# Per-token-tile products of a two-layer hybrid encoder trunk moved from GpSimd to ScalarE

## The chip, the cores and the metric

The kernel runs on one core of a Trainium2 chip. The metric is the device time of one execution in microseconds (us), and the time of a version is the median over several executions. Engines are named as the profile names them: PE is TensorE, DVE is VectorE, ACT is ScalarE, POOL is GpSimd, SP is SyncE.

## The reference

Two layers of an encoder with D = 2048 run over 768 tokens: one request of 256 and one of 512. In each layer an RMS norm and one wide projection feed four groups of heads, four heads each: A (gated delta rule in both directions over chunks), B (differential attention), C (short gated convolution) and M (cross-attention into 256 memory tokens). Their outputs are gated, concatenated, projected, normed and added to the input.

```python
for l in range(DEPTH):                                   # DEPTH = 2
    h = _rmsnorm(x, norm_pre[l])
    (a_qkv, a_dec, a_beta, a_z, b_q, ..., m_q, m_z) = split(h @ w_in[l])
    y_a = _gdn_branch(a_qkv, a_dec, a_beta, a_z, ...)    # group A
    y_b = _diff_branch(b_q, b_k, b_v, b_z, ...)          # group B
    y_c = _conv_branch(c_b, c_c, c_x, c_z, conv_w[l])    # group C
    y_m = _memory_branch(m_q, m_z, mem, ...)             # group M
    y = concat([y_a, y_b, y_c, y_m]) @ w_out[l]
    x = x + _rmsnorm(y, norm_post[l])
# group A, per head and direction, k and q of unit length
decay  = exp(where(tri_incl, g_i - g_j, -inf))           # g: running sum of the decay
a_low  = where(tri_strict, (k * beta) @ k.T * decay, 0)
u      = solve(a_low + eye, v * beta)
```

At the end of a head of A or B its output is normed over the head's 128 columns: every token's row is multiplied by one root of its own.

## The kernel before, in words

**Tiles.** The 768 tokens are 6 token tiles of 128 (`NCH` = 6). A per-head array such as `A`, `U`, `ao` or `bo` has shape [128, 6, 128]: one row of partitions for each token of a tile, six tiles side by side. A factor "per row and token tile" is a small [128, 6] array.

**Projections.** All large products run in split precision: a weight of 512 rows by 128 columns (a quarter) is cast by ACT to a rounded `hi` (L171), DVE subtracts that to get `lo` (L182), and PE multiplies hi and lo by the activations, 24 matmuls for a quarter (L221). `run_jobs` walks over these quarters in a fixed order; quarter i issues the cast of quarter i+4 and, further ahead, its load.

**Head work as tasks.** What the heads do besides projecting is written as generators. Between two quarters `tick` lets the tasks go on by one step, `yield` ends a step. So the small work of several heads is interleaved with the projections in one program order, and each engine executes its part of that order strictly in turn: an instruction that waits for a semaphore holds up all behind it on its engine.

**The three places of the change.** In `head_norm_out` (tasks of A and B) DVE forms the root `hny` in a chain of small operations, the output `ao` or `bo` is multiplied by it (L610), and PE transposes the result (L619), in two groups of four and two token tiles. In `gdn` the masks are multiplied by decays (`gm`, L680; four products of a head, a high and a low part for each of two directions); PE sums them over a triangle (L691), ACT takes the exponential into `A` (L692). Later DVE makes `nD`, a product of beta and key norms (L722, L723), and `U` is `A` times `nD` for both directions (L726).

**A neighbour.** Group M's task runs between them. For each pair of token tiles PE makes scores in a PSUM tile (L1152), DVE their maximum `mmx` (L1155, L1156), ACT two exponentials `mE` (L1159), which are the last readers of that PSUM tile, DVE divides by the sum (L1163, L1165), PE transposes (L1171), ACT and DVE copy the transpose to a high and a low part `mPT` (L1173, L1174), and PE multiplies them by the memory values (L1182). PSUM tiles for these small products come from a pool of four.

Of the kernel before, what the change touches and what calls it, by code (L numbers as in the profile page):

```python
# [12 lines left out]
AF = mybir.ActivationFunctionType  # L13
ALU = mybir.AluOpType
# [4 lines left out]
P = 128  # L19
# [4 lines left out]
NCH = T // P  # L24
# [62 lines left out]
class Trunk:  # L87
# [504 lines left out]
    def head_norm_out(self, o, c, w, st, l, yi):  # L592

        nc = self.nc
        yield 0
        sq = self.sc("hsq")
        nc.scalar.activation(sq[:, :T], o.rearrange("p n c -> p (n c)"), AF.Square)
        yield 0
        so = self.small(NCH, "so")
        nc.vector.tensor_reduce(so, sq[:, :T].rearrange("p (n c) -> p n c", n=NCH), AX.X, ALU.add)  # L600
        yield 0
        if c is not None:
            c2 = self.small(NCH, "c2")
            nc.vector.tensor_tensor(c2, c, c, ALU.mult)
            nc.vector.tensor_tensor(so, so, c2, ALU.mult)
        nc.vector.tensor_scalar(so, so, 1.0 / P, EPS, ALU.mult, ALU.add)  # L606
        r = self.rsqrt(so, NCH, "hn")
        if c is not None:
            nc.vector.tensor_tensor(r, r, c, ALU.mult)
        nc.gpsimd.tensor_tensor(o, o, r.unsqueeze(2).to_broadcast([P, NCH, P]), ALU.mult)  # L610
        while "g" not in st:
            yield 0
        y = st["g"]
        yield (2, 1)
        pts = []
        for off, ln, n0, nn in GROUPS:
            pt = self.psl()
            for n in range(nn):
                nc.tensor.transpose(pt[:, n * P:(n + 1) * P], o[:, n0 + n, :], self.ident)  # L619
            pts.append(pt)  # L620
        for (off, ln, n0, nn), pt in zip(GROUPS, pts):
            nc.vector.scalar_tensor_tensor(y[:, off:off + ln], pt[:, :ln], w, y[:, off:off + ln], ALU.mult, ALU.mult)
        yield from self.store_y(l, yi, y)
# [46 lines left out]
    def gdn(self, l, h, st):  # L670
        nc = self.nc
        while l not in self.dec:
            yield 0
        dec = self.dec[l]
        masks = (self.LE, self.GE)
        gms = []
        for d in range(2):
            gms.append([self.scr("gm") for _ in range(2)])
            for x in range(2):
                nc.gpsimd.tensor_tensor(gms[d][x].rearrange("p (n c) -> p n c", n=NCH),  # L680
                                        masks[d].unsqueeze(1).to_broadcast([P, NCH, P]),
                                        dec["gs"][:, x, 2 * h + d, :].unsqueeze(2).to_broadcast([P, NCH, P]), ALU.mult)
        A = []
        for d in range(2):
            yield (2, 1)
            a = self.sc3("A")
            af = a.rearrange("p n c -> p (n c)")
            for off, ln, n0, nn in GROUPS:
                pt = self.psl()
                for x in range(2):  # L690
                    nc.tensor.matmul(pt[:, :ln], self.maskr[:, d, :], gms[d][x][:, off:off + ln], start=x == 0, stop=x == 1)  # L691
                nc.scalar.activation(af[:, off:off + ln], pt[:, :ln], AF.Exp)  # L692
            sg = 1 - 2 * d
            nc.gpsimd.affine_select(a, a, pattern=[[0, NCH], [sg, P]], compare_op=ALU.is_ge,  # L694
                                    fill=0.0, base=0, channel_multiplier=-sg)
            A.append(a)
        while "k" not in st:
            yield 0
        k = st["k"]
        yield 2  # L700
        ktok = self.sc3("ktok")
        ss = self.small(12, "ss")
        sq = self.sc("ksq")
        for off, ln, n0, nn in GROUPS:
            pt = self.psl()
            for n in range(nn):
                nc.tensor.transpose(pt[:, n * P:(n + 1) * P], k[:, n0 + n, :], self.ident)
            nc.scalar.copy(ktok[:, n0:n0 + nn, :].rearrange("p n c -> p (n c)"), pt[:, :ln])
        nc.scalar.activation(sq[:, :T], ktok.rearrange("p n c -> p (n c)"), AF.Square)
        yield 0  # L710
        nc.vector.tensor_reduce(ss[:, 0:6], sq[:, :T].rearrange("p (n c) -> p n c", n=NCH), AX.X, ALU.add)
        nc.vector.tensor_scalar(ss[:, 0:6], ss[:, 0:6], 4.0 * EPS, None, ALU.add)
        rk = self.rsqrt(ss[:, 0:6], 6, "kn")
        nE = self.small(6, "nE")
        nc.vector.scalar_tensor_tensor(nE, ss[:, 0:6], -0.5, rk, ALU.mult, ALU.mult)
        rk2 = self.small(6, "rk2")
        nc.vector.scalar_tensor_tensor(rk2, rk, -1.0, rk, ALU.mult, ALU.mult)
        nD = self.small(12, "nD").rearrange("p (d n) -> p d n", d=2)
        nDR = self.small(12, "nDR").rearrange("p (d n) -> p d n", d=2)
        U = []  # L720
        for d in range(2):
            nc.vector.tensor_tensor(nD[:, d, :], dec["be"][:, 2 * h + d, :], rk2, ALU.mult)  # L722
            nc.vector.tensor_tensor(nDR[:, d, :], nD[:, d, :], dec["eR"][:, 2 * h + d, :], ALU.mult)  # L723
        for d in range(2):
            u = self.sc3("U")
            nc.gpsimd.tensor_tensor(u, A[d], nD[:, d, :].unsqueeze(2).to_broadcast([P, NCH, P]), ALU.mult)  # L726
            U.append(u)
        yield 0
        while "q" not in st:
            yield 0  # L730
        q = st["q"]
        for p in range(3):
            yield 1
            pt = self.psl()
            p4 = pt.rearrange("p (a n c) -> p a n c", a=2, n=2)
            for j in range(2):
                n = 2 * p + j
                for a, x in enumerate((k, q)):
                    nc.tensor.matmul(p4[:, a, j, :], k[:, n, :], x[:, n, :])  # L739
            for X, a in ((U, 0), (A, 1)):  # L740
                for d in range(2):
                    v = X[d][:, 2 * p:2 * p + 2, :]
                    nc.vector.tensor_tensor(v, p4[:, a], v, ALU.mult)
        inv = Task(self.gdn_inverse(U, st))
        self.tasks.append(inv)
        yield 2
        sq = self.sc("qsq")
        for off, ln, n0, nn in GROUPS:
            pt = self.psl()
            for n in range(nn):  # L750
                nc.tensor.transpose(pt[:, n * P:(n + 1) * P], q[:, n0 + n, :], self.ident)
            nc.scalar.activation(sq[:, off:off + ln], pt[:, :ln], AF.Square)
        yield 0
        nc.vector.tensor_reduce(ss[:, 6:12], sq[:, :T].rearrange("p (n c) -> p n c", n=NCH), AX.X, ALU.add)
        nc.vector.tensor_scalar(ss[:, 6:12], ss[:, 6:12], 4.0 * EPS, None, ALU.add)
        rq = self.rsqrt(ss[:, 6:12], 6, "qn")
        cq = self.small(6, "cq")
        nc.vector.tensor_scalar(cq, rq, P ** -0.5, None, ALU.mult)
        while "v" not in st:
            yield 0  # L760
        v = st["v"]
        yield 2
        nv = self.sc3("nv")
        for off, ln, n0, nn in GROUPS:
            pt = self.psl()
            for n in range(nn):
                nc.tensor.transpose(pt[:, n * P:(n + 1) * P], v[:, n0 + n, :], self.ident)
            nc.vector.tensor_tensor(nv[:, n0:n0 + nn, :], pt[:, :ln].rearrange("p (n c) -> p n c", n=nn),
                                    nE[:, n0:n0 + nn].unsqueeze(2).to_broadcast([P, nn, P]), ALU.mult)
        while "inv" not in st:  # L770
            yield 0
        o = self.sc3("ao")
        yield from self.gdn_scan(h, dec, k, q, ktok, nv, U, A, nD, nDR, o)
        yield from self.head_norm_out(o, cq, self.gnw[:, l:l + 1], st, l, h)
# [774 lines left out]
```

## Time and profile before

| what | value |
|---|---|
| median of 3 executions | 3085.11 us (3083.47 to 3088.78) |
| the profiled execution | 3081.02 us, its span 3079.3 us |
| busy share of the span: PE, DVE, ACT, POOL | 97%, 52%, 29%, 28% |
| mean granted clock of PE | 0.989 of full speed |
| HBM | 87 GB/s over the span |

The span is the time from the first to the last instruction of the profiled execution; 1.7 us of its own time lie around it. Busy shares are means over the whole span. In rows of the trace the first number is the start and the second the duration, in us; "x4" is the number of instructions merged into a row; brackets at the end tell how long the engine had stood idle before the row, and what ended that.

### The profile page before, as it was taken

Reading aid. Unit: us, or ns where it says so; the run is one execution under the profiler, and the core shown is the slowest. Engines: PE = TensorE matmul, PEld = TensorE weight load, DVE = VectorE, ACT = ScalarE, POOL = GpSimd, SP = SyncE. Lnnn points to the kernel's source line nnn. Section 1 sums busy time; section 2 is a strip of 40 time slices with the busy share of each in tenths; the row PEclk is TensorE's granted clock in tenths of the full one; section 3 lists DMA queues with packets and bytes.
Section 4 is the critical chain, followed back from the end, with each engine's and each line's share of the span. In section 5 each row is a group of like instructions: output and inputs, shape, how many; then the busy total and the mean of one; then the engine's idle time right before and its main releaser. Section 6 shows DMA issues by size and latency. Waiting matters only on the chain. (4 is left out here: it accounts for less than half of the span.)

```text
span 3079.3 us, 47114 instructions
## 1 busy us (share of the span) xinstructions
PE 2998.0 (97%) x18606; PEld 2600.5 (84%) x18606; DVE 1610.6 (52%) x2964; ACT 902.2 (29%) x1802; POOL 861.4 (28%) x1070
## 2 busy tenths in 40 slices
PE   8899999999999999999989999999999999999997
PEld 6788888888888888888867888888888888888886
DVE  7755465455355645632596554645463546455236
ACT  6432222222222232421234222322222222334111
POOL 4316114310701250311253260252107014303014
PEclk9999999999999999999999999999999999999998
DMA  7422223122222221531473222221222122224226
GB/s 246 124 69 64 66 58 84 52 64 73 71 55 69 73 61 46 181 96 56 128 241 104 69 61 62 63 79 54 71 75 65 53 69 72 61 74 156 59 66 215
DMA packets 170829, 269.81 MB, mean 88 GB/s; under 512 B 41584, under 2 KB 54128, under 8 KB 170608
## 3 DMA queue, kind: packets, MB, share of 16 engines
q1 hardware_dynamic: 169376, 265.74, 29.1%
q8 instruction: 146, 2.39, 0.3%
q10 hardware_dynamic: 1232, 1.07, 0.1%
q14 instruction: 75, 0.61, 0.1%
HBM read 233.97 MB, written 32.77 MB: 87 GB/s over the span
## 5 line engine op out<-in xcount | busy, mean ns | idle before, releaser
L221 PE MATMUL pp<-h,hi 128*128 128x512 f32 (+1 forms) x9600 | 2178.1, 344 | 9.8 <-ACT h L365 6.2
L221 PEld LDWEIGHTS pp<-h,hi 128*128 128x128 f32 x9600 | 1507.1, 189 | 232.1 <-issue 8.3
L221 PE MATMUL pp<-h,lo 128*128 128x512 f32 (+1 forms) x4800 | 1309.2, 342 | 8.8 <-DVE lo L182 8.8
L182 DVE TENSOR_TENSOR lo<-raw,hi 128x512 fp32r<-128x512 f32 x700 | 607.5, 880 | 742.7 <-ACT hi L171 739.7
L221 PEld LDWEIGHTS pp<-h,lo 128*128 128x128 f32 x4800 | 762.0, 189 | 122.9 <-DVE lo L182 12.4
L171 ACT CAST hi<-raw 128x512 fp32r<-128x512 f32 x700 | 415.9, 618 | 247.0 <-PE pp L221 192.1
L1355 POOL TENSOR_TENSOR acc<-acc,osq 128x768 f32<-128x768 f32 (+2 forms) x36 | 53.7, 1492 | 407.2 <-ACT osq L1348 407.2
L797 POOL TENSOR_TENSOR tl<-ul 48x30 f32<-48x30 f32 (+14 forms) x240 | 136.3, 568 | 94.4 <-DMA ul<-ud 34.3
L799 POOL TENSOR_TENSOR ul<-ul,tl 48x30 f32<-48x30 f32 (+14 forms) x240 | 145.1, 605 | 18.8
L610 POOL TENSOR_TENSOR ao<-ao,hny 128x768 f32<-128x768 f32 x8 | 13.2, 1646 | 481.5 <-DVE so L606 435.8
L1340 DVE TENSOR_SCALAR ys<-pp,npost_s 128x768 f32<-128x768 f32 (+2 forms) x41 | 34.4, 839 | 187.6 <-PE pp L221 187.6
L1073 ACT ACTIVATE E<-s,bmx 128x512 f32<-128x512 f32 (+1 forms) x96 | 58.4, 613 | 235.6 <-DVE bmx L1072 224.8
L648 DVE SCALAR_TENSOR_TENSOR cva<-cv,gconv_s,cva 128x770 f32<-128x770 f32 x96 | 104.5, 1088 | 5.0
L1348 ACT ACTIVATE osq<-pp 128x768 f32<-128x768 f32 (+2 forms) x38 | 25.8, 678 | 260.2 <-DVE ys L1340 260.2
L680 POOL TENSOR_TENSOR gm<-masks_s,gr 128x768 fp32r<-128x768 f32 x32 | 51.8, 1648 | 116.9 <-DVE gr L566 116.9
L726 POOL TENSOR_TENSOR U<-A,nD 128x768 f32<-128x768 f32 x16 | 27.4, 1733 | 166.9 <-DVE nD L722 166.9
L924 ACT ACTIVATE x<-s,nD 128x128 f32<-128x128 f32 x96 | 33.6, 367 | 137.1 <-PE s L922 116.7
L1072 DVE TENSOR_REDUCE bmx<-s 128x1 f32<-128x512 f32 (+1 forms) x96 | 53.2, 596 | 28.9 <-PE s L1069 28.5
L610 POOL TENSOR_TENSOR bo<-bo,hny 128x768 f32<-128x768 f32 x8 | 13.3, 1665 | 186.3 <-DVE hny L298 186.3
L1159 ACT ACTIVATE mE<-s,mmx 128x256 f32<-128x256 f32 x48 | 22.4, 471 | 139.8 <-DVE mmx L1156 131.6
L694 POOL TENSOR_SCALAR_AFFINE_SELECT A<-A 128x768 f32<-128x768 f32 x16 | 14.8, 926 | 171.4 <-ACT A L692 171.4
L587 ACT ACTIVATE gate<-pp 128x768 f32<-128x768 f32 x32 | 26.0, 812 | 125.3 <-PE pp L221 124.6
(304 smaller groups left out, 2703.8 us busy)
## 6 DMA issues: line engine op xcount, KB each, us to landing
raw<-wu SPq DMA_DIRECT2D x472, 256.0 KB, 3.0
raw<-wo SPq DMA_DIRECT2D x164, 256.0 KB, 3.4
raw<-wkv SPq DMA_DIRECT2D x64, 256.0 KB, 4.6
y<-gate SPq DMA_DIRECT2D x24, 384.0 KB, 2.6
mem<-memT SPq DMA_DIRECT2D x32, 256.0 KB, 4.7
x<-xT SPq DMA_DIRECT2D x16, 384.0 KB, 6.9
yl<-y SPq DMA_DIRECT2D x24, 256.0 KB, 5.3
xl<-xT SPq DMA_DIRECT2D x16, 384.0 KB, 4.4
```

Of the source, the lines that this page charges most:

```text
L171: nc.scalar.copy(hi, rf)
L182: nc.vector.tensor_tensor(lo, rf, hi.bitcast(F32), ALU.subtract)
L221: nc.tensor.matmul(job.ps[:, o:o + n], w[:, j, :], job.H[g][k][:, x, :], start=(k == 0 and w is hi and x == 0), stop=(k == KT - 1 and w is ...
L648: nc.vector.scalar_tensor_tensor(a, cb[:, i:i + 770], w[:, i:i + 1], a, ALU.mult, ALU.add)
L680: nc.gpsimd.tensor_tensor(gms[d][x].rearrange("p (n c) -> p n c", n=NCH), masks[d].unsqueeze(1).to_broadcast([P, NCH, P]), dec["gs"][:, x, ...
L797: nc.gpsimd.tensor_tensor(t, ul[:, j + 1:, j:j + 1].to_broadcast([48, m, j]), ul[:, j:j + 1, 0:j].to_broadcast([48, m, j]), ALU.mult)
L799: nc.gpsimd.tensor_tensor(ul[:, j + 1:, 0:j], ul[:, j + 1:, 0:j], t, ALU.add)
L924: nc.scalar.activation(xt[:, ci, :], pb[:, ci * P:(ci + 1) * P], AF.Copy, scale=nD[:, d, n:n + 1])
L1072: nc.vector.tensor_reduce(mx[:, j:j + 1], pts[j][:, :ln], AX.X, ALU.max, negate=True)
L1073: nc.scalar.activation(E[j], pts[j][:, :ln], AF.Exp, bias=mx[:, j:j + 1], accum_out=sm[:, j:j + 1])
L1340: nc.vector.tensor_scalar(st["ys"][m][:, a:b], ps[:, a:b], self.npost[:, l, m:m + 1], None, ALU.mult)
L1355: nc.gpsimd.tensor_tensor(acc[:, o:o + n], acc[:, o:o + n], sq[:, o:o + n], ALU.add)
```

## The change

All 64 POOL products of the three places (32 `gm`, 16 `U`, 8 `ao`, 8 `bo`, each on 128 partitions by 768 elements) become scaled copies on ACT, one for each token tile: 384 instructions of 128 by 128, whose scale is a column of the small array. The `gm` of a direction are now made just ahead of that direction's sum, two tiles at a time, where all four were made before the first.

```diff
-        nc.gpsimd.tensor_tensor(o, o, r.unsqueeze(2).to_broadcast([P, NCH, P]), ALU.mult)
+        for n in range(NCH):
+            nc.scalar.activation(o[:, n, :], o[:, n, :], AF.Copy, scale=r[:, n:n + 1])
...
-        gms = []
-        for d in range(2):
-            gms.append([self.scr("gm") for _ in range(2)])
-            for x in range(2):
-                nc.gpsimd.tensor_tensor(gms[d][x].rearrange("p (n c) -> p n c", n=NCH),
-                                        masks[d].unsqueeze(1).to_broadcast([P, NCH, P]),
-                                        dec["gs"][:, x, 2 * h + d, :].unsqueeze(2).to_broadcast([P, NCH, P]), ALU.mult)
         A = []
         for d in range(2):
+            gm = [self.scr("gm") for _ in range(2)]
+            for x in range(2):
+                for n in range(NCH):
+                    nc.scalar.activation(gm[x][:, n * P:(n + 1) * P], masks[d], AF.Copy,
+                                         scale=dec["gs"][:, x, 2 * h + d, n:n + 1])
             yield (2, 1)
...
         for d in range(2):
             u = self.sc3("U")
-            nc.gpsimd.tensor_tensor(u, A[d], nD[:, d, :].unsqueeze(2).to_broadcast([P, NCH, P]), ALU.mult)
+            for n in range(NCH):
+                nc.scalar.activation(u[:, n, :], A[d][:, n, :], AF.Copy, scale=nD[:, d, n:n + 1])
             U.append(u)
```

The order of instructions on PE, DVE and SP stays as it was. POOL's loses its 64 instructions, and ACT's gains the 384 at the places where the tasks issue them. Three of these places follow, as ACT's queue stands there (engine order, not times).

The first is in the third head of A in the first layer, around `U`. Before, ACT's queue reads:

```order
L708 COPY ktok_6946<-s_6955 128x256
L709 ACTIVATE ksq_6948<-ktok_6946 128x768
L171 CAST hi_6960<-raw_6791 128x512
L171 CAST hi_7026<-raw_6837 128x512
L650 ACTIVATE cv_6937<-cva_6991 128x770
L1159 ACTIVATE mE_7068,msm_7065<-s_7057,mmx_7064 128x256 x2
L171 CAST hi_7071<-raw_6878 128x512
```

And with the change, where numbers behind names and a few line numbers are shifted:

```order
L707 COPY ktok_7046<-s_7055 128x256
L708 ACTIVATE ksq_7048<-ktok_7046 128x768
L171 CAST hi_7060<-raw_6891 128x512
L726 ACTIVATE U_7122<-A_6768,nD_7116 128x128 x6
L726 ACTIVATE U_7129<-A_6877,nD_7116 128x128 x6
L171 CAST hi_7136<-raw_6937 128x512
L651 ACTIVATE cv_7037<-cva_7091 128x770
L1159 ACTIVATE mE_7178,msm_7175<-s_7167,mmx_7174 128x256 x2
L171 CAST hi_7181<-raw_6978 128x512
```

Twelve copies that need `nD` now stand between two `hi` casts, ahead of the exponentials `mE`. The second `hi` is the one whose `lo` stands on DVE directly behind L723 and directly ahead of L1155 and L1156.

The second place is the end of the second head of A and B in the same layer, shortly before that. Before, ACT's queue reads:

```order
L1108 CAST mq_6387<-pp_6251 128x768
L1128 CAST mkvh_6395<-mkv_6224 128x512
L171 CAST hi_6398<-raw_6249 128x512
L171 CAST hi_6463<-raw_6292 128x512
L1159 ACTIVATE mE_6504,msm_6501<-s_6493,mmx_6500 128x256 x2
L171 CAST hi_6507<-raw_6327 128x512
```

With the change:

```order
L1108 CAST mq_6457<-pp_6321 128x768
L1128 CAST mkvh_6465<-mkv_6294 128x512
L171 CAST hi_6468<-raw_6319 128x512
L611 ACTIVATE ao_5827<-ao_5827,hny_6503 128x128 x6
L611 ACTIVATE bo_5393<-bo_5393,hny_6524 128x128 x6
L171 CAST hi_6543<-raw_6362 128x512
L1159 ACTIVATE mE_6584,msm_6581<-s_6573,mmx_6580 128x256 x2
```

Again the second `hi`, whose `lo` on DVE stands directly ahead of L1155, has come behind copies that wait for a DVE chain, those of `bo` for the later one.

The third place is the end of the last head of B in a layer. Before, ACT's queue reads:

```order
L924 ACTIVATE x_11639<-s_11690,nD_9670 128x128 x2
L1173 CAST mPT_11715<-s_11710 128x512
L171 CAST hi_11719<-raw_11515 128x512
L171 CAST hi_11762<-raw_11552 128x512
L597 ACTIVATE hsq_11792<-ao_11141 128x768
```

With the change:

```order
L924 ACTIVATE x_11789<-s_11840,nD_9810 128x128 x2
L611 ACTIVATE bo_10647<-bo_10647,hny_11846 128x128 x6
L1173 CAST mPT_11870<-s_11865 128x512
L171 CAST hi_11874<-raw_11665 128x512
L171 CAST hi_11917<-raw_11702 128x512
```

Here the copy of M's transpose, `mPT`, has come behind the six copies of `bo`.

## Rows read from the trace of the kernel before

**Rows 1.** The page, busy time of the engines and their share of the span.

```profile
PE 2998.0 (97%) x18606; PEld 2600.5 (84%) x18606; DVE 1610.6 (52%) x2964; ACT 902.2 (29%) x1802; POOL 861.4 (28%) x1070
```

**Rows 2.** PE's waits over the span: total us, times, longest.

```profile
PE s L1171 <- DVE mE L1165: 16.6, 10, 2.7
```

**Rows 3.** Groups by line and form on ACT: busy us, mean ns.

```profile
L171 ACT CAST hi<-raw 128x512 fp32r<-128x512 f32 x700 | 415.9, 618 | 247.0 <-PE pp L221 192.1 <-issue 22.4 <-ACT hi L171 20.0
...
L924 ACT ACTIVATE x<-s,nD 128x128 f32<-128x128 f32 x96 | 33.6, 367 | 137.1 <-PE s L922 116.7 <-DVE xr L926 10.2 <-DVE x L926 10.1
```

**Rows 4.** Timeline, 1224 to 1232 us, the end of the first layer's last head.

```profile
1224.03 0.63 ACT L924 ACTIVATE x<-s,nD 128x128 f32<-128x128 f32 x2 [6.50 <-PE s L922]
...
1224.55 0.59 ACT L1173 CAST mPT<-s 128x512 fp32r<-128x512 f32 x1
...
1227.71 0.68 DVE L1174 TENSOR_TENSOR mPT<-s,mPT 128x512 fp32r<-128x512 f32 x1
1227.95 1.47 POOL L610 TENSOR_TENSOR bo<-bo,hny 128x768 f32<-128x768 f32 x1 [30.39 <-DVE hny L298]
...
1228.86 0.48 PE L1182 MATMUL s<-mPT,mkvh 128*128 128x256 f32 x2
```

**Rows 5.** Timeline, 742 to 750 us, around U of the third head.

```profile
742.73 3.42 POOL L726 TENSOR_TENSOR U<-A,nD 128x768 f32<-128x768 f32 x2 [28.96 <-DVE nD L722]
742.86 1.36 DVE L723 TENSOR_TENSOR nDR<-nD,ea 128x6 f32<-128x6 f32 x1
...
744.14 0.68 DVE L182 TENSOR_TENSOR lo<-raw,hi 128x512 fp32r<-128x512 f32 x1
...
745.46 0.72 DVE L1156 TENSOR_SCALAR mmx<-mmx 128x2 f32<-128x2 f32 x1
...
746.27 0.47 ACT L1159 ACTIVATE mE<-s,mmx 128x256 f32<-128x256 f32 x1 [6.54 <-DVE mmx L1156]
...
749.98 0.70 PE L1171 MATMUL s<-masks_s,mE 128*128 128x128 f32 x4 [2.30 <-DVE mE L1165]
```

**Rows 6.** Timeline, DVE, 706 to 708 us, while POOL does nothing.

```profile
707.57 0.17 DVE L1156 TENSOR_SCALAR mmx<-mmx 128x2 f32<-128x2 f32 x1
```

**Rows 7.** Timeline, 682 to 692 us, the norms at a head's end.

```profile
682.83 0.69 DVE L182 TENSOR_TENSOR lo<-raw,hi 128x512 fp32r<-128x512 f32 x1
683.06 1.79 POOL L610 TENSOR_TENSOR bo<-bo,hny 128x768 f32<-128x768 f32 x1 [1.98 <-DVE hny L298]
...
685.43 0.47 ACT L1159 ACTIVATE mE<-s,mmx 128x256 f32<-128x256 f32 x1
...
685.53 0.94 PE L619 MATMUL s<-masks_s,bo 128*128 128x128 f32 x6
...
691.31 0.63 PE L1171 MATMUL s<-masks_s,mE 128*128 128x128 f32 x4 [0.66 <-DVE mE L1165]
```

**Rows 8.** Timeline, 197 to 208 us, the first head's masks and a convolution.

```profile
197.32 7.53 POOL L680 TENSOR_TENSOR gm<-masks_s,gr 128x768 fp32r<-128x768 f32 x4 [59.32 <-DVE gr L566]
197.40 1.83 DVE L646 TENSOR_SCALAR cva<-cv,gconv_s 128x770 f32<-128x770 f32 x1
...
199.26 7.46 DVE L648 SCALAR_TENSOR_TENSOR cva<-cv,gconv_s,cva 128x770 f32<-128x770 f32 x4
...
206.81 0.85 ACT L650 ACTIVATE cv<-cva 128x770 f32<-128x770 f32 x1 [7.52 <-DVE cva L648]
...
207.34 0.86 PE L691 MATMUL s<-gm,maskr 128*128 128x512 f32 x4
```

**Rows 9.** Timeline, 734 to 739 us, a convolution while POOL does nothing.

```profile
734.53 4.26 DVE L648 SCALAR_TENSOR_TENSOR cva<-cv,gconv_s,cva 128x770 f32<-128x770 f32 x4
```

**Rows 10.** Timeline, PE, 60 to 75 us: a long wait.

```profile
68.50 2.07 PE L324 MATMUL s<-dg,masks_s 128*128 128x512 f32 x2 [5.48 <-DVE dg L318]
```

**Rows 11.** Two windows: us, busy of PE, PEld, DVE, ACT, POOL, granted clock, DMA.

```profile
66.20:72.90 6.70, 4.41 (x8) 2.82 (x9) 5.35 (x14) 3.10 (x5) 0.89 (x1) 0.50 0.22 75
...
1028.80:1032.10 3.30, 3.30 (x14) 3.06 (x14) 2.24 (x7) 1.62 (x3) 0.00 (x0) 0.50 0.33 101
```

More of the change, by code (lines that the diff above doesn't have):

```diff
@@ L690, in gdn @@
                 for x in range(2):
-                    nc.tensor.matmul(pt[:, :ln], self.maskr[:, d, :], gms[d][x][:, off:off + ln], start=x == 0, stop=x == 1)
+                    nc.tensor.matmul(pt[:, :ln], self.maskr[:, d, :], gm[x][:, off:off + ln], start=x == 0, stop=x == 1)
                 nc.scalar.activation(af[:, off:off + ln], pt[:, :ln], AF.Exp)
```

## The prediction

> **What bounds the kernel now.** I read the busy line first: PE works in 97% of the span, no other engine in more than 52% [rows 1]. So time is the projections' matmuls plus what PE waits, and the change adds no work to PE. Then I read PE's waits by line: ten of them, 16.6 us together, the longest 2.7, are L1171 waiting for the divided exponentials `mE` [rows 2]. In the timeline six of these ten stand a few us behind `U` of the second, third and fourth head of each layer (2.1 to 2.7 us, one of 2.30 in [rows 5]), and the other four behind the norms at the start of the third and fourth head (about 0.6, one in [rows 7]). So group M's chain max, exp, divide already ends last at two of the places where the change puts work on ACT. I then read both places instruction by instruction, and the order of ACT's queue after the change against them.
>
> **What one copy costs.** The nearest row is L924, also a copy by a scale per row, 128 by 128, but from PSUM: 0.367 us each [rows 3], two together 0.63 [rows 4], so one starts 0.263 behind the other. The new copies read SBUF: a 512-wide rounding cast takes 0.59 from PSUM [rows 4] and 0.618 from SBUF [rows 3], 0.03 more. That gives 0.295; I take **s = 0.30 us** for a copy in a series. The ends are 0.263 (SBUF costs nothing) and 0.367 (no overlap at all). All 384 are 115 us of ACT, an engine that is busy 29%; the volume alone costs nothing. What costs is that ACT executes in order: a copy that waits for DVE's scalar holds all behind it.
>
> **U, second to fourth head, six places.** POOL starts on U at 742.73, when DVE has made nD [rows 5]. ACT can start there too: 12 copies end at 742.73 + 3.60 = 746.33. The `hi` cast queued behind them had been long done; now it ends 0.62 later, at 746.95. Its `lo` stands on DVE ahead of L1155, so DVE stops there until 746.95, where it was at 744.14 before: 2.81 late. Against that, L1156 gets faster. It took 0.72 while POOL worked on U, and 0.17 where POOL did nothing [rows 5, 6]: 0.55 back. The second L723 (1.36 under POOL) gets faster as well, but that is worth nothing, since DVE then waits for `hi` longer. So `mE`, the divide and PE's L1171 come 2.81 - 0.55 = 2.26 later, and PE, which waits there already, waits that much more. As a formula 12 s - 1.34. Six places: **+13.6 us** (10.9 to 18.4).
>
> The rule of the Trainium skill that speaks for the change bears on this place. "SBUF — State Buffer", section "SBUF: two separate sides", says that VectorE with two SBUF inputs and GpSimd reading SBUF exclude each other for a whole instruction, while ScalarE has a port of its own. The 1.36 and 0.72 us of small DVE operations under U agree. By that rule alone the place would get shorter by what DVE gets back; by the queue it gets longer; this is the first rival below.
>
> **Norms at a head's end, four places.** POOL starts `bo` at 683.06 [rows 7], when hny is there. Six copies end at 684.86, the `hi` behind them at 685.48; its `lo` was at 682.83, so it is 2.65 late, and with the 0.55 of L1156 `mE` is 2.10 late. Here PE meets it twice. The second `mE` ends at 685.43 + 0.47 = 685.90, and PE's second group of `bo` transposes (L619, from 685.53 on, six in 0.94) needs the PSUM tile that `mE` reads last; it goes on at about 686.0, so there is no slack. PE waits about 2.1 there. The wait of 0.66 at L1171 then vanishes: PE comes 2.1 later, and DVE's work ahead of it is no longer slowed by POOL's masks. Net 2.10 - 0.66 = 1.44 each, 6 s - 0.36. Four places: **+5.8** (4.9 to 7.4).
>
> **End of the last head of B, two places.** ACT's `mPT` (at 1224.55 before) is now behind `bo`, whose root is there at 1227.95 [rows 4]: 1227.95 + 1.80 + 0.59 = 1230.34, then L1174 0.68, to 1231.02. PE needs that low part for its second matmul of L1182, at about 1229.07. So PE waits 1.95, twice: **+3.9** (3.5 to 4.7).
>
> **What costs nothing.** `U` of the first head has no `mE` behind it. The masks' decays are there from the layer's start, so their copies wait for nothing and only delay casts; a cast is issued four quarters ahead of PE, and a quarter lasts about 4.2 us (24 of the matmuls whose merged groups fill the timeline). The last `ao` of a layer delays activations' casts by under 3 us, and PE catches up on its lead. One place is close: the first head's masks. DVE's convolution there ran under POOL's masks (7.53 us for four): L646 took 1.83 and four steps of L648 7.46 [rows 8], against 4.26 for four steps alone [rows 9]. Now ACT's `cv` (L650) stands ahead of the copies. With L646 at no more than one step (1.07) the convolution ends at 197.40 + 1.07 + 4.26 = 202.73, cv 0.85 later, 12 copies at 207.2; PE's L691 is at 207.34 [rows 8]. So nothing is lost (at s = 0.367, 0.6 us over two layers).
>
> Sum of the waits: 13.6 + 5.8 + 3.9 = **23.3** (19.3 to 31.1).
>
> **The clock.** Behind a wait PE's granted clock can fall from 1.0 to 0.50, that is from 2.4 to 1.2 GHz. Behind a wait of 5.48 us [rows 10] the window 66.20 to 72.90 has 0.50; behind the third U wait of a layer (2.2 us) the window 1028.80 to 1032.10 has it [rows 11], and so in the second layer; behind the other four U waits the clock stays at 1.0. In a stretch of 3.3 to 3.4 us at half clock PE loses 1.7 us. After the change the six U waits are 4.4 to 5 us, nearer to 5.48 than to 2.2; I give each one such stretch, four more than now: 6.8. Six new waits of about 2 us get them as those of 2.1 to 2.7 do now, two of six: 3.4. Together **+10.2**. Lowest: no wait brings one, and the two of before go: -3.4. Highest: 6.7 us at half clock (3.35 lost) behind each of the six, and 1.7 behind each of the six new: 20.1 + 10.2 - 3.4 = 26.9.
>
> So the profiled execution would go from 3081.0 to 3081.0 + 23.3 + 10.2 = 3114.5. The median is 4.1 above the profiled execution; on it, 3085.1 + 33.5 = **3119**.
>
> **Rivals.**
> *POOL's hold on DVE is what counts (faster).* If a copy in series took less than 0.11 us, 12 s - 1.34 would be negative: M's chain would then come earlier, because DVE gets L723 and L1156 back. At the limit each of the six waits shrinks by 1.3 and both half-clock stretches go: 3085.1 - 7.9 - 3.4 = 3074. For it: DVE under POOL is slower by 1.2 and 0.55 us at that very place, and by 4 us in the first convolution. Against it: L924's 0.263 is more than twice the limit. The same would follow if ACT got nD much earlier, but nD comes off DVE's own chain, which POOL does not slow before U begins.
> *The copies only delay casts (no change).* PE's waits for `lo` are short and rare today since casts run quarters ahead, and ACT has 71% of its time free. Then 3085, give or take 6. Against it: the order rows show that `lo` of the delayed cast stands ahead of M's chain on DVE, which PE does wait for.
> *The first head's masks come late as well (slower still).* If the convolution keeps its old length, cv ends at 207.66 and 12 copies end at 211.3, where PE wants them at 207.34: 3.9 for each layer, 3119 + 8 = 3127. It decides once the convolution gives back less than about 3.9 us. Against it: without POOL the same four steps take 4.26.
>
> **How the numbers follow.** The forecast gets 0.77, faster 0.07, no change 0.08, slower still 0.08. What this kernel's measurement tells from no change is about 0.2%, 6 us. The range covers the forecast and the last rival: lowest 3085.1 + 19.3 - 3.4 = 3101, less the 1.6 to 3 us by which executions differ, 3098; highest 3085.1 + 31.1 + 26.9 = 3143, plus 3.7 (the highest of the three runs over their median), 3147. The other two cases, 15 in 100, are left out. Faster 0.07, same 0.08, slower 0.85.
>
> **What would show it.** In the profile of after, U's copies start within 0.2 us of nD, follow each other at about 0.30, and the `hi` behind them ends 4.2 us after nD. PE's wait at L1171 behind U is 4.4 to 5.0 us in six places. A new wait of PE at L619 for ACT's `mE` (about 2.1, four times) and one at L1182 for L1174 (about 2, twice) appear, and the four waits of 0.6 at L1171 are gone. L723, L1156 and the first convolution are at their undisturbed times. The mean granted clock falls slightly below 0.989. I would be wrong if copies follow each other much faster than in L924, if PE's waits at the six places stay at 2.3, or if half-clock stretches become long behind the new waits.

## The result and the profile after

The changed kernel takes 3106.95 us (median of four, 3104.56 to 3107.71) against 3084.65 before: a ratio of 1.0069, 95% interval 1.0051 to 1.0086. That is 22 us slower, where 34 were forecast, and inside the range. The profiled execution has a span of 3102.8 us, 23.5 more than before, and the mean granted clock is 0.986.

The busy line of the page, to be set beside [rows 1], and the groups of the new copies:

```profile
PE 3003.4 (97%) x18606; PEld 2605.7 (84%) x18606; DVE 1567.2 (51%) x2964; ACT 1012.4 (33%) x2186; POOL 754.4 (24%) x1006
...
L682 ACT ACTIVATE gm<-masks_s,gr 128x128 fp32r<-128x128 f32 x192 | 57.9, 396 | 0.0
...
L726 ACT ACTIVATE U<-A,nD 128x128 f32<-128x128 f32 x96 | 29.0, 389 | 61.4 <-DVE nD L721 61.4
```

POOL gave back 107 us, DVE 43, and ACT took 110: no engine but PE is near its limit, and PE's own matmuls take 5.4 us longer while their number is the same. So 18.1 of the 23.5 us are idle time of PE. Its waits by line (total, times, longest), beside [rows 2]:

```profile
PE s L1171 <- DVE mE L1165: 26.2, 6, 4.8
...
PE s L620 <- ACT mE L1159: 3.0, 4, 0.8
...
PE s L1182 <- ACT mPT L1173: 2.4, 2, 1.2
...
PE s L1182 <- DVE mPT L1174: 0.9, 3, 0.3
```

Before, ten waits at L1171 made 16.6 us, about 14.2 of them in the six behind U. Now these six alone make 26.2: 12.0 more. The four of 0.6 at the norms are gone, and four of 0.75 at the transposes of `bo` (L620, L619 before) have come. The end of the last head of B waits at L1182, as forecast, about 1.6 us in each layer (the third DVE wait there, 0.2 us, is at another head).

The timeline of the changed kernel around U of the third head shows the chain, beside [rows 5]:

```profile
742.23 0.28 PE L1152 MATMUL s<-mkvh,mq 128*128 128x256 f32 x1
...
746.19 3.63 ACT L726 ACTIVATE U<-A,nD 128x128 f32<-128x128 f32 x12 [9.36 <-DVE nD L721]
...
746.46 0.17 DVE L722 TENSOR_TENSOR nDR<-nD,ea 128x6 f32<-128x6 f32 x1
...
749.72 0.60 ACT L171 CAST hi<-raw 128x512 fp32r<-128x512 f32 x1
...
750.36 0.69 DVE L182 TENSOR_TENSOR lo<-raw,hi 128x512 fp32r<-128x512 f32 x1 [3.73 <-ACT hi L171]
...
751.69 0.17 DVE L1156 TENSOR_SCALAR mmx<-mmx 128x2 f32<-128x2 f32 x1
751.95 0.47 ACT L1159 ACTIVATE mE<-s,mmx 128x256 f32<-128x256 f32 x1 [0.87 <-DVE mmx L1156]
...
755.66 1.11 PE L1171 MATMUL s<-masks_s,mE 128*128 128x128 f32 x4 [4.23 <-DVE mE L1165]
```

ACT waits 9.36 us for nD with a long-ready cast behind it, then makes twelve copies in 3.63 us: (3.63 - 0.389) / 11 = 0.295 us apart. DVE stands 3.73 us for `hi`. L722 (L723 before) and L1156 are back at 0.17. PE waits 4.23 us where it waited 2.30.

In the windows behind these six waits and behind the last head, the granted clock (third number from the end) is half:

```profile
470.30:477.10 6.80, 4.74 (x19) 4.48 (x20) 5.34 (x13) 2.69 (x6) 0.00 (x0) 0.50 0.30 80
753.60:760.40 6.80, 4.74 (x19) 4.45 (x20) 5.41 (x13) 2.77 (x6) 0.00 (x0) 0.50 0.28 77
...
1036.90:1043.70 6.80, 5.19 (x21) 4.81 (x22) 5.40 (x14) 2.32 (x5) 0.00 (x0) 0.50 0.44 138
1241.70:1245.10 3.40, 3.40 (x13) 2.92 (x12) 0.93 (x2) 1.34 (x2) 0.00 (x0) 0.50 0.51 160
2013.10:2016.50 3.40, 3.40 (x16) 3.21 (x15) 2.13 (x5) 1.62 (x3) 0.00 (x0) 0.50 0.48 137
2296.40:2299.80 3.40, 3.40 (x15) 3.21 (x14) 2.37 (x7) 1.62 (x3) 0.00 (x0) 0.50 0.36 110
2576.30:2583.10 6.80, 4.88 (x19) 4.58 (x20) 5.40 (x14) 2.63 (x6) 0.00 (x0) 0.50 0.49 162
```

PE worked 26.35 us at 1.2 GHz in the six windows behind U, and 3.40 behind the last head of the first layer. In a stretch at half clock PE gets through half the matmuls (13 for 25, last section), so half of that is lost: 13.2 and 1.7, where the two windows of before lost 3.3.

### The profile page after: what moved, and what is told of

It reads as the page before. It is cut to its first block, busy times and chain, and to the rows that moved or that the text cites. A ratio compares the mean times of both kernels' runs of the same rounds, so it can differ in the third digit from the quotient of the medians.

```text
span 3102.8 us, 47378 instructions
## 1 busy us (share of the span) xinstructions
PE 3003.4 (97%) x18606; PEld 2605.7 (84%) x18606; DVE 1567.2 (51%) x2964; ACT 1012.4 (33%) x2186; POOL 754.4 (24%) x1006
## 3 DMA queue, kind: packets, MB, share of 16 engines
q10 hardware_dynamic: 1232, 1.07, 0.1%
## 5 line engine op out<-in xcount | busy, mean ns | idle before, releaser
L182 DVE TENSOR_TENSOR lo<-raw,hi 128x512 fp32r<-128x512 f32 x700 | 592.2, 858 | 842.6 <-ACT hi L171 840.7
L785 POOL COPY cd<-U 32x192 f32<-32x192 f32 x32 | 18.0, 561 | 304.8 <-DVE U L743 303.7
L924 ACT ACTIVATE x<-s,nD 128x128 f32<-128x128 f32 x96 | 33.5, 366 | 133.1 <-PE s L922 112.7
L332 POOL TENSOR_TENSOR h<-yl,h 128x256 fp32r<-128x256 f32 (+1 forms) x28 | 32.2, 1173 | 130.9 <-DMA yl<-y 106.0
L682 ACT ACTIVATE gm<-masks_s,gr 128x128 fp32r<-128x128 f32 x192 | 57.9, 396 | 0.0
L1094 ACT ACTIVATE bo<-s,brs 128x128 f32<-128x128 f32 x48 | 17.6, 366 | 114.4 <-PE s L1092 114.4
L726 ACT ACTIVATE U<-A,nD 128x128 f32<-128x128 f32 x96 | 29.0, 389 | 61.4 <-DVE nD L721 61.4
```

Source lines behind the costliest of these rows:

```text
L182: nc.vector.tensor_tensor(lo, rf, hi.bitcast(F32), ALU.subtract)
L682: nc.scalar.activation(gm[x][:, n * P:(n + 1) * P], masks[d], AF.Copy, scale=dec["gs"][:, x, 2 * h + d, n:n + 1])
L924: nc.scalar.activation(xt[:, ci, :], pb[:, ci * P:(ci + 1) * P], AF.Copy, scale=nD[:, d, n:n + 1])
```

## The experiments

All medians below stand against the kernel before on the same chip (3084.2 in the first four, 3084.5 in the next four, 3084.8 in the last).

### U alone on ACT

Masks and norms as before, U's loop from the change:

```diff
-            nc.gpsimd.tensor_tensor(u, A[d], nD[:, d, :].unsqueeze(2).to_broadcast([P, NCH, P]), ALU.mult)
+            for n in range(NCH):
+                nc.scalar.activation(u[:, n, :], A[d][:, n, :], AF.Copy, scale=nD[:, d, n:n + 1])
```

> Only U goes to ACT, as 96 copies; the masks and the norms stay on POOL. Theory (the queue): the loss is where copies that wait for DVE's chain stand in ACT's order ahead of the hi cast whose lo precedes M's chain on DVE. Then U alone carries nearly all: six waits of PE at L1171 of 4.2 to 4.8 us behind U and half-clock stretches behind them, as in the changed kernel, where these six places lose 21 us. Time about 3106 (3102 to 3109). Rival (the volume of work given to ACT, 110 us in 384 instructions): U's 96 carry a quarter of the 22 us, about 3090.

3104.02 us, ratio 1.0061 (1.0048 to 1.0074): 19.8 us of the 22 come with a quarter of the copies. The volume theory is out. PE's waits at M's transposes:

```profile
PE s L1172 <- DVE mE L1166: 28.7, 10, 4.6
```

Six of these stand behind U and make 26.3 us, as in the changed kernel (26.2); the four of 0.6 at the norms are still there.

### All but U on ACT

Against the changed kernel:

```diff
-            for n in range(NCH):
-                nc.scalar.activation(u[:, n, :], A[d][:, n, :], AF.Copy, scale=nD[:, d, n:n + 1])
+            nc.gpsimd.tensor_tensor(u, A[d], nD[:, d, :].unsqueeze(2).to_broadcast([P, NCH, P]), ALU.mult)
```

> Masks and norms go to ACT as in the changed kernel, U stays on POOL. Theory (the queue): PE's waits behind U are 2.1 to 2.7 us again; what stays is the end of the last head of B (about 5 us for both layers, wait and clock), the masks of the second head (1 us), and next to nothing at the norms. Time about 3090 (3085 to 3093). Rival (volume): 288 of 384 instructions carry 17 of the 22 us, about 3101.

3089.29 us, ratio 1.0012 (1.0003 to 1.0020): 5 us. The waits behind U are as before:

```profile
PE s L1170 <- DVE mE L1164: 14.1, 6, 2.9
```

3.0 us stand at L620 and 3.3 at the matmuls behind `mPT` (L1181 in this run). The two parts, U alone and all but U, add up to 24.9, near the whole.

### U's copies one step of the tasks later

```diff
+        yield 0
         for d in range(2):
             u = self.sc3("U")
...
             U.append(u)
-        yield 0
```

> All as in the changed kernel, but U's copies are issued one step of the tasks later: on ACT they then stand behind mE and ahead of the next two hi casts, the first of which gives the lo that stands on DVE ahead of L653, L1163 and L1165. The order on PE, DVE and SP is unchanged. Theory A (any hi whose lo stands ahead of M's chain on DVE carries the delay): mE comes earlier, the divide doesn't; U's copies end near mE's end + 3.5 us, then hi, lo, L653 and the divide; PE's six waits stay at about 4 us, time 3103 to 3108. Theory B (what counts is that mE itself stands behind the copies on ACT): with mE free and DVE not held by POOL the six waits fall under 1 us and the half-clock stretches go, about 3076.

3104.85 us, ratio 1.0064 (1.0052 to 1.0077): theory A. The waits at L1171 are 24.4 us. The third head's timeline:

```profile
748.23 0.47 ACT L1159 ACTIVATE mE<-s,mmx 128x256 f32<-128x256 f32 x1 [4.83 <-DVE mmx L1156]
...
749.14 3.62 ACT L727 ACTIVATE U<-A,nD 128x128 f32<-128x128 f32 x12
...
752.65 1.13 ACT L171 CAST hi<-raw 128x512 fp32r<-128x512 f32 x2
753.30 0.69 DVE L182 TENSOR_TENSOR lo<-raw,hi 128x512 fp32r<-128x512 f32 x1 [5.16 <-ACT hi L171]
...
755.44 1.12 PE L1171 MATMUL s<-masks_s,mE 128*128 128x128 f32 x4 [3.79 <-DVE mE L1165]
```

`mE` starts 3.7 us earlier than in the changed kernel (748.23 against 751.95, with PE within 0.1 us of each other there), and PE gains 0.4 of it. The exponential was never what had to be early; a cast for PE's next quarters, whose `lo` DVE must make before M's divide, carries the delay.

### bo alone on ACT

```diff
-        nc.gpsimd.tensor_tensor(o, o, r.unsqueeze(2).to_broadcast([P, NCH, P]), ALU.mult)
+        if c is None:
+            for n in range(NCH):
+                nc.scalar.activation(o[:, n, :], o[:, n, :], AF.Copy, scale=r[:, n:n + 1])
+        else:
+            nc.gpsimd.tensor_tensor(o, o, r.unsqueeze(2).to_broadcast([P, NCH, P]), ALU.mult)
```

> Only bo's product goes to ACT; ao, U and the masks stay on POOL. In the changed kernel the norms cost next to nothing, where 1.4 us each were forecast. Theory: the forecast took bo's root at its old time, but part of DVE's chain to it (L294, 1.35 us under POOL's ao product) gets 1.2 us shorter once ao is off POOL. With ao left on POOL that gain is gone: PE waits about 2.0 us at the bo transposes in four places and loses the 0.6 at L1171, and the end of the last head costs 2.0 us in each layer with some half-clock stretches: 5.6 + 5, about 3095. Rival (the wait at the transposes is short for another reason, such as the PSUM tile being freed earlier): 0.8 us at each place as in the changed kernel, about 3090.

3121.91 us, ratio 1.0119 (1.0104 to 1.0135): 38 us slower with 48 copies, worse than the whole change. Neither answer had that. The timeline at the end of the second head:

```profile
680.90 1.47 POOL L614 TENSOR_TENSOR ao<-ao,hny 128x768 f32<-128x768 f32 x1 [108.98 <-DVE so L606]
681.05 1.35 DVE L294 TENSOR_SCALAR hny<-hny 128x6 int32<-128x6 int32 x1
...
682.33 5.75 POOL L684 TENSOR_TENSOR gm<-masks_s,gr 128x768 fp32r<-128x768 f32 x4
682.43 1.39 DVE L296 TENSOR_TENSOR hnt<-hny 128x6 f32<-128x6 f32 x1
...
683.85 1.39 DVE L297 SCALAR_TENSOR_TENSOR hnt<-hnt,so 128x6 f32<-128x6 f32 x1
...
685.28 1.40 DVE L298 SCALAR_TENSOR_TENSOR hny<-hnt,hny 128x6 f32<-128x6 f32 x1
...
686.71 1.39 DVE L296 TENSOR_TENSOR hnt<-hny 128x6 f32<-128x6 f32 x1
...
689.20 1.86 ACT L612 ACTIVATE bo<-bo,hny 128x128 f32<-128x128 f32 x6 [14.24 <-DVE hny L298]
...
689.65 1.35 PE L623 MATMUL s<-masks_s,bo 128*128 128x128 f32 x4 [2.67 <-ACT bo L612]
...
694.27 0.69 PE L623 MATMUL s<-masks_s,bo 128*128 128x128 f32 x2 [3.26 <-ACT mE L1163]
```

In the kernel before, POOL's own `bo` product, waiting for the root, stood ahead of the next head's masks and kept them off. With `bo` on ACT the four masks start right behind `ao`, and each of the next four steps of DVE's chain to the root, 0.17 us by itself, takes about 1.39. Counted from PE's scores, the root comes about 5 us later than before; PE waits 2.7 for `bo` and 3.3 more for `mE`, and so at all four places:

```profile
PE s L623 <- ACT mE L1163: 13.0, 4, 3.3
PE s L623 <- ACT bo L612: 10.7, 4, 2.7
```

At each of the four the granted clock falls to 0.50 around the first wait and stays there for 10.2 us. The expectation was right that POOL slows that chain and missed which POOL work would.

### ao on POOL, masks and bo on ACT

Against the run with all but U on ACT (`c` is None for `bo`):

```diff
-        for n in range(NCH):
-            nc.scalar.activation(o[:, n, :], o[:, n, :], AF.Copy, scale=r[:, n:n + 1])
+        if c is None:
+            for n in range(NCH):
+                nc.scalar.activation(o[:, n, :], o[:, n, :], AF.Copy, scale=r[:, n:n + 1])
+        else:
+            nc.gpsimd.tensor_tensor(o, o, r.unsqueeze(2).to_broadcast([P, NCH, P]), ALU.mult)
```

> Against the run with all but U on ACT: only ao goes back to POOL (masks and bo on ACT, U on POOL). Theory: PE's short wait at the bo transposes (0.75 us) comes from bo's root being early, since nothing on POOL slows DVE's chain to it. With ao on POOL one step of that chain (L294) takes 1.35 us again, the root comes 1.2 later, and PE's wait there is about 2.0 us in four places: 3089.3 + 4.8 = 3094, a little more if half-clock stretches follow. Rival (the root's chain is not what sets that wait): 0.8 us and 3089 as before.

3096.56 us, ratio 1.0043 (1.0030 to 1.0056), 7 us above all but U on ACT. PE's waits at the transposes:

```profile
PE s L623 <- ACT mE L1161: 7.6, 4, 2.0
```

1.9 us each where it was 0.75: the theory. And against the run with `bo` alone it is 25 us faster, with nothing changed but the masks, which are on ACT here and made a direction at a time. Together with the four steps of 1.39 us under the masks in that run's timeline, this shows the masks on POOL to be the cause there.

### U's copies two steps later

```diff
+        yield 0
+        if h:
+            yield 0
         for d in range(2):
             u = self.sc3("U")
...
             U.append(u)
-        yield 0
```

> All on ACT as in the changed kernel, but U's copies of the second to fourth head are issued two steps later: on ACT they stand behind mE and one more hi cast, the one whose lo stands ahead of the divide. The order on PE, DVE and SP is unchanged. Theory (only hi casts whose lo stands ahead of M's chain on DVE count): the chain is no longer behind U at all, and DVE is not held by POOL either, so mE and the divide come about 1.7 us earlier than before; PE's six waits fall from 2.4 to under 1 us, without half-clock stretches. Time about 3075 (3072 to 3079). Rival (ACT's load as such, or U late for its reader L743): the waits move to L739 or later places, time 3085 or more.

3074.51 us, ratio 0.997 (0.996 to 0.998): all 384 copies on ACT, and 10 us faster than before. Third head's timeline, and the waits:

```profile
746.61 0.61 ACT L171 CAST hi<-raw 128x512 fp32r<-128x512 f32 x1
...
747.12 3.62 ACT L729 ACTIVATE U<-A,nD 128x128 f32<-128x128 f32 x12
...
747.26 0.69 DVE L182 TENSOR_TENSOR lo<-raw,hi 128x512 fp32r<-128x512 f32 x1 [1.66 <-ACT hi L171]
```

```profile
PE s L1173 <- DVE mE L1167: 3.4, 6, 1.0
```

Against the run with U one step later, one cast has changed sides with the twelve copies, and six waits of 4.1 on average have become six of under 0.6. (`if h` leaves the first head at one step; no `mE` stands behind its U.)

### U two steps later, bo on POOL

Against the last run:

```diff
-        for n in range(NCH):
-            nc.scalar.activation(o[:, n, :], o[:, n, :], AF.Copy, scale=r[:, n:n + 1])
+        if c is not None:
+            for n in range(NCH):
+                nc.scalar.activation(o[:, n, :], o[:, n, :], AF.Copy, scale=r[:, n:n + 1])
+        else:
+            nc.gpsimd.tensor_tensor(o, o, r.unsqueeze(2).to_broadcast([P, NCH, P]), ALU.mult)
```

> As the run with U two steps later, but bo's product back on POOL (masks, ao and U on ACT). Theory: the end of the last head loses its wait at L1182 (2 us twice, with half-clock stretches), and the hi at a head's end is no longer behind bo, so PE's 0.75 at the bo transposes goes, with no wait in its place, since neither ao nor the masks slow the chain to bo's root: about 3067 (3063 to 3071). Rival (bo on POOL holds DVE where M's chain needs it, 0.55 at L1156, and PE waits 0.6 at L1171 as in the kernel before): 3071 to 3075.

3065.89 us, ratio 0.9941 (0.9928 to 0.9953). PE waits 3.7 us at the transposes behind U in all (six times); the waits at `bo`'s transposes and at L1182 are gone.

### U two steps later and nothing else

Against the kernel before; masks and norms stay on POOL:

```diff
+        yield 0
+        if h:
+            yield 0
         for d in range(2):
             u = self.sc3("U")
-            nc.gpsimd.tensor_tensor(u, A[d], nD[:, d, :].unsqueeze(2).to_broadcast([P, NCH, P]), ALU.mult)
+            for n in range(NCH):
+                nc.scalar.activation(u[:, n, :], A[d][:, n, :], AF.Copy, scale=nD[:, d, n:n + 1])
             U.append(u)
-        yield 0
```

> The kernel before with nothing but U on ACT, two steps later. Theory: six waits at L1171 of 2.4 us fall under 1 us and the half-clock stretches behind them go, the four waits of 0.6 at the norms stay: 3084.2 - 10 - 3.4 = 3071 (3067 to 3075). Rival (POOL, free earlier, goes on with other work sooner and holds DVE at another place): little gain, 3080 or more.

3067.52 us, ratio 0.9950 (0.9938 to 0.9963): 17 us faster than before; 13 were expected. PE's waits at M's transposes:

```profile
PE s L1174 <- DVE mE L1168: 6.5, 10, 1.0
```

The six behind U make 3.9 us of that, for 14.2 before, and behind none of them is the clock halved. In the third head `mE` starts 6.08 us after PE begins M's scores (742.84 - 736.76), where it was 7.78 (746.27 - 738.49): 1.7 earlier, which is what the second L723 and L1156 took longer under POOL's U (1.19 + 0.55). So one small edit has nearly all that the best version has; the times of the two overlap (3063.67 to 3066.53 and 3065.66 to 3070.63), and a difference of a few us between them is not shown. Whether U two steps later but still on POOL would gain as much was not tried: that too would keep POOL off DVE at these two steps.

### The masks alone on ACT

The kernel before with the change's middle hunk, the loop over `gm`, which also makes each direction's masks just ahead of its sum:

```diff
-                nc.gpsimd.tensor_tensor(gms[d][x].rearrange("p (n c) -> p n c", n=NCH),
...
+                for n in range(NCH):
+                    nc.scalar.activation(gm[x][:, n * P:(n + 1) * P], masks[d], AF.Copy,
+                                         scale=dec["gs"][:, x, 2 * h + d, n:n + 1])
```

> Only the masks gm go to ACT (192 of the 384 copies); U, ao and bo stay on POOL. Theory: their decays wait for nothing, so their copies only delay casts that PE wants quarters later, and the first head's still come in time, as DVE's convolution is no longer slowed; PE loses about 0.5 us at the second head's masks in each layer and saves the four waits of 0.6 at L1171. Time as before, 3083 (3081 to 3087). Rival (volume on ACT): half of the 22 us, about 3095; rival (first head's masks late): 8 us, about 3092.

3083.99 us, ratio 0.9997 (0.9988 to 1.0006): 192 copies, half of all, change nothing that can be measured.

## Why the prediction was right, and where not

**The price of a copy** was 0.295 us in a series, for 0.30 taken. The Trainium skill's page "ScalarE: Activation LUTs", section "What ACT_TABLE_LOAD costs", gives 186 ns plus 0.833 ns an element, 93 more for a scale from a pointer and 93 overlap: by it, an estimate of 0.293. The trace agrees (0.295).

**U, six places:** 12.0 us of added wait for 13.6 forecast, by the mechanism forecast. In the third head ACT could start 0.28 us earlier than POOL did, counted from PE's L1152 (746.19 - 742.23 = 3.96; before 742.73 - 738.49 = 4.24), which is most of the missing 0.33 there.

```profile
738.49 0.28 PE L1152 MATMUL s<-mkvh,mq 128*128 128x256 f32 x1
```

The rival in which POOL's hold on DVE decides has its effect (L723, now L722, and L1156 at 0.17), but it pays only where the casts stand ahead of U: with U two steps later that gain is what makes the kernel faster. The rule of the Trainium skill's page "SBUF — State Buffer", section "SBUF: two separate sides", that only VectorE and GpSimd exclude each other agrees with the 1.39 us steps under the masks; by itself it gave the wrong sign, since the order in ACT's queue weighed more. Two of the slowed operations, L1156 (0.72) and L294 (1.35), read only one array, so the condition in the prediction's words, two SBUF inputs, does not cover them.

**Norms, four places:** the step that failed. The forecast had `mE` 2.10 us late and a net loss of 1.44 each, 5.8 in all; measured are waits of 0.75 at L620 less 0.6 at L1171, 0.6 us in all. It took the root of `bo` at its old time. In the trace before, one step of its chain ran under POOL's product of `ao`:

```profile
679.61 1.47 POOL L610 TENSOR_TENSOR ao<-ao,hny 128x768 f32<-128x768 f32 x1 [109.09 <-DVE so L606]
679.76 1.35 DVE L294 TENSOR_SCALAR hny<-hny 128x6 int32<-128x6 int32 x1
```

The changed kernel has the same L294 at 0.17, so the copies of `bo` start 1.2 us earlier than reckoned, and PE's wait at L620 is short:

```profile
683.31 0.17 DVE L294 TENSOR_SCALAR hny<-hny 128x6 int32<-128x6 int32 x1
...
685.38 1.87 ACT L611 ACTIVATE bo<-bo,hny 128x128 f32<-128x128 f32 x6 [0.44 <-DVE hny L298]
...
690.46 0.44 PE L620 MATMUL s<-masks_s,bo 128*128 128x128 f32 x2 [0.83 <-ACT mE L1159]
```

2.10 - 1.18 = 0.92, and the row at L620 has 0.83. The run with `ao` back on POOL brings the wait to 1.9. The forecast had given DVE its time back at L1156 and not at L294, the earlier step in the chain to the root.

**The end of the last head of B** was sized right, 4.0 for 3.9, though PE's wait splits in two: 1.23 for the high part of `mPT`, 0.34 for the low one, with a matmul between. The low part's matmul came 2.0 us late (at 1240.71; L935 right ahead of it runs 9.65 us later than before, at 1238.15, which would have put this matmul at 1238.7), for 1.95, and the second layer's waits are as long:

```profile
1239.37 0.56 ACT L1173 CAST mPT<-s 128x512 fp32r<-128x512 f32 x1
...
1240.71 0.39 PE L1182 MATMUL s<-mPT,mkvh 128*128 128x256 f32 x1 [0.34 <-DVE mPT L1174]
```

**The masks** cost nothing, as forecast, and the first head's were as close as it said: ready at 206.98, wanted at 207.41.

```profile
203.37 3.61 ACT L682 ACTIVATE gm<-masks_s,gr 128x128 fp32r<-128x128 f32 x12
...
207.41 0.85 PE L690 MATMUL s<-gm,maskr 128*128 128x512 f32 x4
```

**The clock:** 10.2 forecast. Behind the six U waits 13.2 are lost where 3.3 were before, 9.9 for 6.8; behind the new waits 1.7 for 3.4. Together 11.6. The size was right and its split was not: all six U waits have a half-clock stretch, as forecast, but four of them last 6.8 us, part of which lies in the wait. That the sum came out is in part luck: the two stretches of before, from which it counts, are those of one execution, and other kernels with U waits as long had three to five (last section).

These places sum to 12.0 + 0.6 + 4.0 + 11.6 = 28 us, 4.7 more than the span grew. Most of that is clock elsewhere: in the half-clock stretches at 66 to 136 us, at 1548 to 1674 us and in the last 22 us PE works 24.7 us, where it worked 32.9 before, which gives 4.1 back. Whether the change has a part in that was not settled. Against the 33.5 of the forecast, the norms are 5.2 short, U 1.6 and these other places 4.7, while the clock behind the named waits is 1.4 over.

## What to carry to other kernels

Ask of every operation moved to an in-order engine not what it costs there but what it waits for, and what behind it some third engine needs next; here a weight cast with quarters of lead became urgent, because DVE had to consume it before a softmax that PE was waiting for. Moving the same twelve copies behind that cast and the next one like it turned 20 us lost into 17 gained; behind the first alone they gained nothing. And when an engine is taken off another's neck, follow the freed chain from its first step, and look at what the freed queue will start early: it can hold the same neighbour longer than before.

## What the runs showed of the hardware

A DVE operation on 128 by 6 elements, 0.17 us by itself, took 1.32 to 1.40 us when it came up just behind the start of a POOL multiplication of 128 by 768. A chain of four such steps (1.39, 1.39, 1.40, 1.39) and four POOL operations (5.75 us) ran in lockstep, one step for each.

The half clock does not follow from a wait's length alone. With all but U on ACT, the third head's wait behind U is 2.25 us, as it was before (2.30), and yet the clock behind it is halved, where before it was not (first fence: all but U on ACT; second: before):

```profile
753.60:757.00 3.40, 3.40 (x13) 2.92 (x12) 3.37 (x8) 0.92 (x2) 0.00 (x0) 0.50 0.27 77
```

```profile
750.50:753.90 3.40, 3.40 (x25) 3.10 (x24) 2.85 (x8) 1.62 (x3) 0.00 (x0) 1.00 0.34 111
```

PE's row has 13 matmuls there and 25 before, in the same 3.4 us. In the one profiled execution of each kernel, the six waits behind U were followed by half clock as follows:

| kernel | U waits, us | followed by half clock |
|---|---|---|
| before | 2.15 to 2.66 | 2 of 6 |
| all but U on ACT | 1.99 to 2.87 | 5 of 6 |
| `bo` alone on ACT | 2.00 to 2.66 | 4 of 6 |
| `ao` on POOL, masks and `bo` on ACT | 2.26 to 2.68 | 3 of 6 |
| masks alone on ACT | 2.10 to 2.55 | 5 of 6 |
| the change, U alone, U one step later | 3.79 to 4.84 | 18 of 18 |
| U two steps later, alone or with all | 0.28 to 0.99 | 0 of 12 |

So each wait of some 2 us carries a chance of losing another 1.7, here 19 times in 30. What decides it was not tried.
